# The front of a two-layer decoder step re-staged (a split x tile, squares summed on TensorE), with a convolution, gate chunks, squares and the last stores moved

## The chip, the core and the metric

The kernel runs on one core of a Trainium2 chip. The metric is the device time of one execution in microseconds; the figure for the kernel before is the median of 3 runs. Names used below: PE is TensorE (matmuls), DVE is VectorE, ACT is ScalarE, POOL is GpSimd, SP is SyncE, which issues most of the transfers. PSUM is the memory that matmuls accumulate in; it is divided into banks of 512 fp32 columns.

## The reference, cut to what matters

Two layers (an SSD layer, then a causal pooling layer) over 1024 prompt tokens and 8 x 8 sample tokens, width 1024, and a final RMSNorm. Everything is fp32.

```
def rmsnorm(x, g):
    return x * lax.rsqrt(jnp.mean(x * x, axis=-1, keepdims=True) + EPS) * g
...
    sc = jax.nn.silu(c)
    for i in range(DEPTH):                       # DEPTH = 2
        mod = sc @ ada_w[i] + ada_b[i]
        shift, scale, gate = jnp.split(mod, 3, axis=-1)
        hn = rmsnorm(x, norm_g[i]) * (1.0 + scale[:, None]) + shift[:, None]
        if i % 2 == 0:
            zxbcdt = hn @ w_in                   # gates z, x/B/C and dt
            conv = conv_b + sum(xp[:, k:k + L] * conv_w[k] for k in range(4)); silu(conv)
            y = ssd_scan(...);  out = grouped_rmsnorm(y * silu(z)) @ w_out
        else:
            u, z = split(hn @ w_in)              # windows of 2, 4, 8, 16 tokens summed over u
            out = (pooled @ w_group * ch_scale * silu(z)) @ w_out
        x = x + (1.0 + gate[:, None]) * out
    y = rmsnorm(x, final_norm_g)
```

## The kernel before, in words

Activations lie channel-major: `x` is 8 tiles (k = 0 to 7) of 128 channels by 1088 tokens (1024 prompt, 64 sample). A projection runs over three token chunks `CH` of 368, 368 and 352 columns. Each fp32 factor is held as a rounded part and a remainder (`hh` and `hl` for activations, `wh` and `wl`, or `w` and `w`, for weights), and one product is three matmuls (`mm1`, L189 to L192: hh x wh, hl x wh, hh x wl). ACT makes the rounded part (a copy), DVE or POOL the remainder (a subtraction).

**The front** (`setup`, `front`). SP loads the conditioning `cT`, the eight x tiles, the table `vec` (conv weights, biases, adaLN bias and norm gains), the constants `kc` (with a 9-column selection matrix), `wdt`, and then the adaLN weights, eight blocks of two 512 KB halves, and the input weights `wr`. SP stops at a transfer when eight are under way until the oldest has landed. Meanwhile PE runs 62 matmuls on a tile of ones (`warm`). ACT squares each x tile (L1411, L1415), DVE adds the squares into `rst` (L1416), PE sums `rst` over the 128 channels by a matmul with ones (L302) into `ms`, and ACT takes Ln (L305) and Exp (L318): `rst` is then 1/rms of each token. adaLN block 0 (`ada_block`): eight matmuls of the two halves into a PSUM bank (L261), a copy to `mp` (L266), two selection matmuls (L270), and DVE makes `shf` and `scl` of x tile 0 (L280, L281). `modulate` makes `hh` and `hl` of a tile: DVE x*scl*rst (L325), ACT the rounded `hh` with the shift (L331), DVE the remainder `hl` (L332); the 64 sample columns go through four short operations of their own (L338 to L342). A loop over k then runs 18 matmuls for each x tile into six PSUM banks (two weight tiles `ws`, three chunks, called mm and p in the trace), four matmuls of `pdt` (L1451, the step sizes dt), and the adaLN block of a later tile. What PE executes is strictly in the order in which a scheduler has put it; `issue_after` ties an instruction behind another.

**The conv of tile 12** (`conv`, called for group 6, beside the output product of group 5): a first term on ACT, three taps on DVE (L368), tanh on ACT and two closing multiplications on DVE (L370, L372). Around it DVE also writes `gl`, the remainders of the gated activations (L806), which matmuls L835 wait for.

**The start of the pooling layer.** PE computes two channel tiles u (names pl) and a gate tile z chunk by chunk; `z_tile` is a gate chunk. DVE meanwhile prepares T matrices and remainders (`t`, `hl`, L1006), weight remainders (`w`, L184) and the window sums of `w_sums` (`ws`, L930, L935). The products that follow (`st`, L1078 to L1080) belong to a seven-product (Strassen-like) block scheme.

**The end.** `squares` adds the squares of x for the final norm beside the last output blocks (L1785, L1786). In the last quarter of the tokens the four x tiles that are finished last have their squares kept in `sqs` and summed by PE one by one; then Ln, Exp, and `scale` multiplies the eight tiles by 1/rms and the gain, six on DVE (L1805) and two on POOL (L1803), and stores them two by two on SP's queue (L1806).

## Time and profile before

| what | before |
| --- | --- |
| median of 3 runs (lowest, highest) | 1586.11 us (1586.0, 1587.76) |
| the profiled execution: its own time, its span | 1586.18 us, 1584.0 us |
| PE busy in the span | 1568.2 us, 99% |
| DVE busy | 1302.7 us, 82% |
| ACT busy, POOL busy | 790.8 us, 528.4 us |
| first projection matmul (L190) starts | 24.48 us |
| last matmul of the kernel ends | 1575.88 us |

The profile is one execution on the chip. Its span runs from the first to the last instruction, and 2.18 us of the execution lie outside it. PE is busy for 99% of the span, so the time changes where PE waits, where it does work that could go away, and at both ends. The end of a matmul is modelled, so a start-to-start distance is a better measure of pace than the idle time shown.

### The profile page before, as it was taken

How to read it: one execution, taken by the hardware profiler on the slowest of the kernel's cores; microseconds unless marked ns; L12 is line 12 of the kernel's file. 1: busy time of each engine (PE TensorE's matmuls, PEld its weight loads, DVE VectorE, ACT ScalarE, POOL GpSimd, SP SyncE). 2: the span in 40 equal slices, each digit the busy share in tenths (PEclk: the TensorE clock that was granted, in tenths of full speed). 3: DMA queues.
4: the chain of work that ended last, by engine and by line, in shares of the span. 5: the costliest groups of instructions: out<-in, count | busy, mean ns of one | idle time of the engine just before them, and what ended most of it. 6: DMA issues, size and time to landing. Idle time of an engine off the chain costs nothing.

```text
span 1584.0 us, 30719 instructions
## 1 busy us (share of the span) xinstructions
PE 1568.2 (99%) x11946; PEld 1504.7 (95%) x11946; DVE 1302.7 (82%) x2152; ACT 790.8 (50%) x1512; POOL 528.4 (33%) x558
## 2 busy tenths in 40 slices
PE   9999999999999999999999999999999999999997
PEld 7899999999999899989999999999999999999997
DVE  6874789887899999889888858998889777667886
ACT  6663344466666666665456338533333233233364
POOL 0133556522322413221211242576566530000241
PEclk9999999999999999999999999999999999999999
DMA  9422232355555565678999432232333379565783
GB/s 357 167 102 92 89 113 75 113 186 177 172 165 174 171 198 159 220 256 297 332 340 316 161 134 64 83 126 98 117 116 115 105 252 364 140 180 178 165 168 124
DMA packets 122304, 275.57 MB, mean 174 GB/s; under 512 B 18192, under 2 KB 59312, under 8 KB 122160
## 3 DMA queue, kind: packets, MB, share of 16 engines
q1 hardware_dynamic: 117840, 259.79, 47.9%
q0 software_dynamic: 4032, 12.72, 4.7%
q8 instruction: 94, 1.54, 0.4%
q10 hardware_dynamic: 288, 1.11, 0.2%
q14 instruction: 50, 0.41, 0.1%
HBM read 201.12 MB, written 70.23 MB: 171 GB/s over the span
## 4 chain that ended last, share of the span: by engine, by line
PE 89%; DVE 5%; issue 3%; DMA 2%; ACT 1%; POOL 0%; SPq 0%; DVEq 0%; ACTq 0%; POOLq 0%
PE st L1079 11%; PE st L1080 11%; PE st L1078 11%; PE mm L190 11%; PE mm L191 11%; PE mm L192 11%; PE op L1298 3%; PE op L1299 3%; PE op L1297 3%; PE y L645 2%; PE S L623 2%; PE y L649 2%; PE tr L584 1%; PE am L261 1%; PE tr L581 1%
## 5 line engine op out<-in xcount | busy, mean ns | idle before, releaser
L1080 PE MATMUL st<-hh,w 128*128 128x272 f32 x832 | 240.2, 289 | 0.0
L1078 PE MATMUL st<-hh,w 128*128 128x272 f32 x832 | 240.0, 289 | 0.0
L1079 PE MATMUL st<-hl,w 128*128 128x272 f32 x832 | 240.0, 288 | 0.0
L1080 PE MATMUL st<-t,w 128*128 128x272 f32 x624 | 179.6, 288 | 0.5 <-DVE w L184 0.5
L1079 PE MATMUL st<-t,w 128*128 128x272 f32 x624 | 179.3, 287 | 0.4 <-DVE t L1006 0.4
L1078 PE MATMUL st<-t,w 128*128 128x272 f32 x624 | 179.6, 288 | 0.0
L190 PE MATMUL mm<-hh,wh 128*128 128x368 f32 (+1 forms) x528 | 178.9, 339 | 0.0
L191 PE MATMUL mm<-hl,wh 128*128 128x368 f32 (+1 forms) x528 | 174.0, 330 | 0.0
L192 PE MATMUL mm<-hh,wl 128*128 128x368 f32 (+1 forms) x528 | 173.3, 328 | 0.0
L1078 PEld LDWEIGHTS st<-hh,w 128*128 128x128 f32 x832 | 156.8, 188 | 0.0
L1079 PEld LDWEIGHTS st<-hl,w 128*128 128x128 f32 x832 | 156.7, 188 | 0.0
L1080 PEld LDWEIGHTS st<-hh,w 128*128 128x128 f32 x832 | 156.4, 188 | 0.0
L182 ACT ACTIVATE w<-wr 128x512 fp32r<-128x512 f32 x104 | 65.0, 629 | 165.2 <-PE st L1080 136.2
L631 POOL TENSOR_TENSOR hd<-h,cd 128x256 f32<-128x256 f32 x56 | 46.1, 823 | 290.4 <-DVE h L632 138.4
L1297 PE MATMUL op<-b,w 128*128 128x272 f32 x448 | 129.4, 289 | 0.0
L1298 PE MATMUL op<-b,w 128*128 128x272 f32 x448 | 128.9, 288 | 0.4 <-DVE b L1226 0.4
L1299 PE MATMUL op<-b,w 128*128 128x272 f32 x448 | 129.0, 288 | 0.0
L190 PE MATMUL mm<-gh,wh 128*128 128x368 f32 (+1 forms) x372 | 125.3, 338 | 0.0
L192 PE MATMUL mm<-gh,wl 128*128 128x368 f32 (+1 forms) x372 | 122.3, 329 | 0.0
L191 PE MATMUL mm<-gl,wh 128*128 128x368 f32 (+1 forms) x372 | 122.0, 328 | 0.1
L1080 PEld LDWEIGHTS st<-t,w 128*128 128x128 f32 x624 | 117.3, 188 | 0.7 <-DVE w L184 0.7
L1079 PEld LDWEIGHTS st<-t,w 128*128 128x128 f32 x624 | 117.2, 188 | 0.6 <-DVE t L1006 0.6
(310 smaller groups left out, 4603.1 us busy)
## 6 DMA issues: line engine op xcount, KB each, us to landing
wr<-win SPq DMA_DIRECT2D x48, 512.0 KB, 3.8
wr<-pin SPq DMA_DIRECT2D x32, 512.0 KB, 3.7
acb<-acd SPq DMA_DIRECT2D x60, 256.0 KB, 5.1
wr<-pout SPq DMA_DIRECT2D x28, 512.0 KB, 3.8
x<-x1d SPq DMA_DIRECT2D x24, 544.0 KB, 6.3
x1d<-x SPq DMA_DIRECT2D x22, 544.0 KB, 4.5
wr<-pout POOLq DMA_DIRECT2D x20, 512.0 KB, 5.6
x<-xT SPq DMA_DIRECT2D x16, 544.0 KB, 8.1
```

What stands on the lines that cost most here:

```text
L182: self.last_hi = self.nc.scalar.activation(hi, src, AF.Copy)
L190: nc.tensor.matmul(ps[:, :n], hi[:, k, :], ah[:, a:a + n], start=first, stop=False)
L191: nc.tensor.matmul(ps[:, :n], hi[:, k, :], al[:, a:a + n], start=False, stop=False)
L192: nc.tensor.matmul(ps[:, :n], lo[:, k, :], ah[:, a:a + n], start=False, stop=last)
L623: nc.tensor.matmul(S[:, 256 * i:256 * i + 256], Bt, xde.rearrange("p r q -> p (r q)"), start=True, stop=True)
L631: nc.gpsimd.tensor_tensor(out=hd, in0=h[-1], in1=cd.unsqueeze(2).to_broadcast([P, 4, 64]), op=ALU.mult)
L1078: nc.tensor.matmul(ps[c][:, :QUART], hi[:, k], xh[:, t], start=(k == 0), stop=False)
L1079: nc.tensor.matmul(ps[c][:, :QUART], hi[:, k], xl[:, t], start=False, stop=False)
L1080: nc.tensor.matmul(ps[c][:, :QUART], lo[:, k], xh[:, t], start=False, stop=(k == 3))
L1297: nc.tensor.matmul(ps[:, :QUART], hi[:, k], xh, start=k == 0, stop=False)
L1298: nc.tensor.matmul(ps[:, :QUART], hi[:, k], xl, start=False, stop=False)
L1299: nc.tensor.matmul(ps[:, :QUART], lo[:, k], xh, start=False, stop=k == 7)
```

## The change

The front is written anew. The load of `cT` (145 columns) carries the selection matrix, the adaLN biases and the norm gains in one load too, so that `vec` and `kc` are not needed at the start. x tile 1 is loaded on ACT's queue. x tile 7 comes in two loads (368 and 720 columns) that stand around the second half of adaLN block 0; the first two weight tiles come in two parts each, the first k = 0, 1 alone. Squares of x tiles 0, 2, 4 and 7 go to PE as they are (a ones matmul for each chunk and tile, L1468 of the changed kernel); DVE adds only those of 3, 5 and 6 to tile 1's in `rst`. The roots are taken chunk by chunk, the first of them between the halves of adaLN block 0. The weights are split in three parts, the last on POOL. Tiles 0 and 1 are modulated in three chunks; the products of the sample columns with `rst` are on POOL, for tile 0 the rest of its sample chain too. `pdt` of a tile runs a step later, the last four together at the end. `warm` issues 14 and then 4, 4, 3, 4 matmuls, before 62 and 8.

Elsewhere: the closing of conv tile 12 goes behind the `gl` of group 5's product; gate chunk 1 of the first pooling tile moves behind the third u chunk; the first window sums are tied behind other DVE work; `squares` goes behind the last block's preparation; the last quarter's squares of three tiles are added on DVE instead of PE; and the last stores are eight, one for each tile, alternately on SP's and ACT's queues.

```
 setup:
-        nc.sync.dma_start(ct, io["cT"])
+        nc.sync.dma_start(first, io["cT"])
         for k in range(8):
             t = self.slots.get("x")
-            nc.sync.dma_start(t, io["xT"][k])
+            if k == 7:
+                a = CH[0][1]
+                self.ada_load(0, (0,))
+                nc.sync.dma_start(t[:, :a], io["xT"][k][:, :a])
+                self.ada_load(0, (1,))
+                nc.sync.dma_start(t[:, a:], io["xT"][k][:, a:])
+            else:
+                (nc.scalar if k == 1 else nc.sync).dma_start(t, io["xT"][k])
-        nc.sync.dma_start(self.vec, io["vec"])
-        nc.sync.dma_start(self.kc, io["kc"])
+        self.first_load(0, 2)
-        self.warm(62)
+        self.warm(14)
...
 front:
+            for k in range(7):
+                sq = rst if k == 1 else self.raw_tile()
+                for a, n in CH if k == 6 else ((0, TOK),):
+                    nc.scalar.activation(sq[:, a:a + n], xs[k][:, a:a + n], AF.Square)
+                if k in (0, 2, 4):
+                    for c in range(3):
+                        mm = add_up(c, sq, k)
+                    with after(mm):
+                        self.warm((4, 0, 4, 0, 3)[k], "y")
+                elif k > 1:
+                    for a, n in CH if k == 6 else ((0, TOK),):
+                        added = nc.vector.tensor_tensor(out=rst[:, a:a + n], in0=rst[:, a:a + n], in1=sq[:, a:a + n], op=ALU.add)
...
         for k in range(8):
-            if k < 6:
-                self.ada_first(k + 2)
-            for a, n in CH if k == 0 else ((0, TOK),):
+            for a, n in CH if k < 2 else ((0, TOK),):
                 last = self.modulate(0, k, xs[k], rst, hi, lo, a, n, xs[k][:, a:a + n])
...
+            if k > 1:
+                with after(self.mod_hi.ins):
+                    if k == 2:
+                        for f in firsts:
+                            f[2](4, 8)()
+                    unrounded(k - 1)
...
+            if 0 < k < 5:
+                with after(mm.ins):
+                    mm = step_sizes(k - 1)
...
 modulate:
-            eng = nc.gpsimd if l and k % 2 == 0 else nc.vector
-            eng.tensor_tensor(out=t[:, pn:n], in0=x[:, s], in1=rst[:, s], op=ALU.mult)
+            eng = nc.gpsimd if k % 2 == 0 and (l or k == 0) else nc.vector
+            if l:
+                eng.tensor_tensor(out=t[:, pn:n], in0=x[:, s], in1=rst[:, s], op=ALU.mult)
...
 conv, tile 12 (op_hi and op_lo are the last gh and gl of the output product):
+        if ti == 2 * BESIDE[-1]:
+            with self.tc.issue_after(self.row_evict):
+                tap(1)
+            self.taps_late = lambda: [tap(k) for k in (2, 3)]
+            self.conv_close = close
+            return
...
                     with self.tc.issue_after(self.op_hi), self.tc.issue_after(self.op_lo):
                         self.gate_late()
+                        self.conv_close()
...
 w_sums and the pooling layer's start:
-            with self.tc.issue_after(self.t_last) if p < PLAIN and step == 1 else contextlib.nullcontext():
+            with self.tc.issue_after({1: self.lows[5], 2: self.t_new}[step]) if p == 0 and step < 4 else contextlib.nullcontext():
...
             if c == 1:
-                for i in range(2):
-                    z_tile(0, wz, i, CH[i])
-        z_tile(0, wz, 2, CH[2])
+                z_tile(0, wz, 0, CH[0])
+        for i in (1, 2):
+            z_tile(0, wz, i, CH[i])
...
 the end:
         def squares(d, c):
-            if d and c == 0:
+            with self.tc.issue_after(self.last_block[0]), self.tc.issue_after(self.last_block[1]):
+                if d and c == 0:
...
-                    t = sqs[:, QUART * d:QUART * d + QUART]
-                    nc.scalar.activation(t, x[d][:, a:a + QUART], AF.Square)
-                    sq.append(t)
+                    if d < 3:
+                        square(d, QUART, QUART)
+                    else:
+                        nc.scalar.activation(sqs[:, :QUART], x[d][:, a:a + QUART], AF.Square)
...
-        scale(QUART, QUART, p1, ((4, 5), (6, 7), (0, 1), (2, 3)), (4, 6))
+        scale(QUART, QUART, p1, ((5, 7, 0, 4), (1, 2, 6, 3)), (4, 6), (nc.sync, nc.scalar))
```

PE's order at the start of the program, before: the ones matmuls of `warm`, the three sums of `rst` (ms), adaLN block 0 (am; the last row of it selects through kc), and the first projection matmuls.

```order
L245 MATMUL warm_205<-ones 128x128 x62
L302 MATMUL ms_312<-rst_284,ones 128x368
L302 MATMUL ms_316<-rst_284,ones 128x368
L302 MATMUL ms_320<-rst_284,ones 128x352
L261 MATMUL am_328<-ada_324,scp 32x256 x4
L261 MATMUL am_328<-ada_326,scp 32x256 x4
L270 MATMUL am_328<-kc,mp_337 128x9 x2
L245 MATMUL warm_353<-ones 128x128 x8
L190 MATMUL mm_381<-hh_407,w_13_345 128x368
L190 MATMUL mm_382<-hh_407,w_13_345 128x368
L191 MATMUL mm_381<-hl_408,w_13_345 128x368
```

PE's order at the same place in the changed kernel, from behind the sums of x tile 4 on: mm_238 to mm_240 are the three chunks' sums, raw_287 the squares of x tile 7, ambank the bank of the adaLN blocks.

```order
L1468 MATMUL mm_238<-rst_237,ones 128x368
L292 MATMUL ambank<-ada_194,scp 32x256 x4
L1468 MATMUL mm_238<-raw_287,ones 128x368
L292 MATMUL ambank<-ada_197,scp 32x256 x4
L1468 MATMUL mm_239<-rst_237,ones 128x368
L1468 MATMUL mm_240<-rst_237,ones 128x352
L302 MATMUL ambank<-ct,mp_301 128x9 x2
L1468 MATMUL mm_239<-raw_287,ones 128x368
L1468 MATMUL mm_240<-raw_287,ones 128x352
L272 MATMUL warm_327<-ones 128x128 x4
L190 MATMUL mm_349<-hh_355,w_12_314 128x368
L191 MATMUL mm_349<-hl_356,w_12_314 128x368
```

The sum of chunk 0 closes between the two halves of adaLN block 0, and the sums of chunks 1 and 2 close behind its selection.

ACT's order in the changed kernel, from the modulation of x tile 0 (hh_355; x_179 is x tile 0, x_181 tile 1) to the next adaLN copy (mp_393): rst_237 is the root, w_14 a weight part.

```order
L1472 ACTIVATE rst_237<-mm_240,eps 128x352
L363 ACTIVATE hh_355<-x_179,shf_229 128x368
L350 ACTIVATE rst_237<-rst_237 128x352
L376 ACTIVATE hh_355<-x_179 128x64
L299 ACTIVATE mp_393<-ambank 128x256
L363 ACTIVATE hh_355<-x_179,shf_229 128x288
L363 ACTIVATE hh_419<-x_181,shf_229 128x368 x2
```

The copy mp_393 and the last chunk of tile 0 stand behind the sample columns' hh (128x64), which needs the end of the last root and three operations on POOL.

DVE's order at the first products st of the pooling layer, before: hl are activation remainders, ws window sums, w weight remainders, u and t operands of the products.

```order
L1006 TENSOR_TENSOR hl_11503<-x_10259,hh_11502 128x544
L930 TENSOR_TENSOR ws_12404<-u_11751 128x1222
L184 TENSOR_TENSOR w_12158<-sw_12149,w_12158 128x512
L184 TENSOR_TENSOR w_12169<-wr_12029,w_12169 128x512
L930 TENSOR_TENSOR ws_12406<-ws_12404 128x1220
L935 TENSOR_TENSOR ws_12406<-ws_12406,kc 128x3
L184 TENSOR_TENSOR w_12201<-sw_12149,w_12201 128x512
L1089 TENSOR_TENSOR u_12161<-st_12204,u_12167 128x272
L1006 TENSOR_TENSOR t_12135<-x_10372,t_12135 128x544
```

And in the changed kernel:

```order
L1060 TENSOR_TENSOR hl_11483<-x_10239,hh_11482 128x544
L184 TENSOR_TENSOR w_12138<-sw_12129,w_12138 128x512
L184 TENSOR_TENSOR w_12149<-wr_12009,w_12149 128x512
L184 TENSOR_TENSOR w_12181<-sw_12129,w_12181 128x512
L1144 TENSOR_TENSOR u_12141<-st_12184,u_12147 128x272
L1060 TENSOR_TENSOR t_12115<-x_10352,t_12115 128x544
L1144 TENSOR_TENSOR u_12141<-st_12185,u_12147 128x272
L184 TENSOR_TENSOR w_12212<-wr_12009,w_12212 128x512
L984 TENSOR_TENSOR ws_12384<-u_11731 128x1222
L1144 TENSOR_TENSOR u_12147<-st_12215,u_12147 128x272
L984 TENSOR_TENSOR ws_12386<-ws_12384 128x1220
```

The two window sums moved from ahead of the weight remainders and of t to behind them.

## Rows read from the trace of the kernel before

**Rows 1.** The page: busy time of each engine, share of the span, instructions.

```profile
PE 1568.2 (99%) x11946; PEld 1504.7 (95%) x11946; DVE 1302.7 (82%) x2152; ACT 790.8 (50%) x1512; POOL 528.4 (33%) x558
```

**Rows 2.** Chain that ended last, 14 to 26 us: start, duration, what.

```profile
17.26 0.46 DVE rst L1416
...
18.68 0.58 ACT rst L305
...
19.28 0.51 ACT rst L318
...
21.51 1.17 DVE x L338 x8
```

**Rows 3.** Timeline of ACT, 12 to 24 us.

```profile
12.60 1.11 ACT L1415 ACTIVATE raw<-x 128x1088 f32<-128x1088 f32 x1 [0.30 <-DMA x<-xT]
13.96 1.11 ACT L1415 ACTIVATE raw<-x 128x1088 f32<-128x1088 f32 x1 [0.25 <-DMA x<-xT]
...
21.57 0.38 ACT L266 ACTIVATE mp<-am 128x256 f32<-128x256 f32 x1
...
23.82 1.11 ACT L331 ACTIVATE hh<-x,shf 128x368 fp32r<-128x368 f32 x2 [0.65 <-DVE x L325]
```

**Rows 4.** Timeline of PE, steps of the front: start, duration, operation.

```profile
24.48 0.95 PE L190 MATMUL mm<-hh,w 128*128 128x368 f32 x2
...
45.42 0.43 PE L190 MATMUL mm<-hh,w 128*128 128x368 f32 x1
...
50.55 0.44 PE L190 MATMUL mm<-hh,w 128*128 128x368 f32 x1
...
63.84 0.44 PE L190 MATMUL mm<-hh,w 128*128 128x368 f32 x1
...
67.68 0.44 PE L190 MATMUL mm<-hh,wh 128*128 128x368 f32 x1
```

**Rows 5.** Timeline of PE, 17 to 22 us: sums, adaLN block 0.

```profile
17.76 2.10 PE L302 MATMUL ms<-rst,ones 128*128 128x368 f32 x6 [0.76 <-DVE rst L1416]
...
20.86 0.64 PE L261 MATMUL am<-ada,scp 128*32 128x256 f32 x8 [0.44 <-DMA ada<-adaA]
```

**Rows 6.** Stretches of warm matmuls: length, busy PE, PEld (count), granted clock.

```profile
1.06:4.80 3.74, 3.74 (x17) 3.74 (x18) 1.00 0.73 187
4.80:6.80 2.00, 2.00 (x20) 2.00 (x19) 1.00 1.00 405
```

**Rows 7.** Groups by shape on POOL, 955 to 1000 us: busy, mean ns.

```profile
L339 POOL TENSOR_TENSOR x<-x,scl 128x64 f32<-128x64 f32 x4 | 1.6, 414 | 0.1
```

**Rows 8.** Waits of PE, 685 to 737 us: total, times, longest.

```profile
PE mm L835 <- DVE gl L806: 1.1, 2, 0.8
```

**Rows 9.** Timeline of DVE, 696 to 716 us.

```profile
699.56 1.22 DVE L370 SCALAR_TENSOR_TENSOR xbc<-raw,raw 128x1024 f32<-128x1024 f32 x1
```

**Rows 10.** Waits of PE, 955 to 1030 us.

```profile
PE st L1080 <- DVE w L184: 0.5, 1, 0.5
PE st L1079 <- DVE t L1006: 0.4, 1, 0.4
PE pl L192 <- DVE wl L145: 0.3, 1, 0.3
```

**Rows 11.** Waits of PE, 1545 to 1553 us.

```profile
PE op L1298 <- DVE b L1226: 0.4, 1, 0.4
```

**Rows 12.** Chain that ended last, from 1573 us.

```profile
1574.03 1.85 PE ms L304 x8
```

**Rows 13.** Timelines of ACT, DVE, POOL at the end; last transfers issued.

```profile
1574.14 0.43 ACT L1843 ACTIVATE sq<-x 128x272 f32<-128x272 f32 x1 [1.97 <-DVE x L1282]
...
1576.85 2.54 DVE L1805 SCALAR_TENSOR_TENSOR y<-x,vec,ms 128x272 f32<-128x272 f32 x6 [2.74 <-ACT ms L1792]
...
1577.36 1.49 POOL L1803 TENSOR_TENSOR y<-x,rst 128x272 f32<-128x272 f32 x2 [6.59 <-ACT rst L318]
...
yT<-y SPq DMA_DIRECT2D x4, 272.0 KB, 2.3
```

More of the change, by code (lines that the diff above doesn't have):

```diff
@@ L191, in mm1 @@
         nc.tensor.matmul(ps[:, :n], hi[:, k, :], al[:, a:a + n], start=False, stop=False)
-        nc.tensor.matmul(ps[:, :n], lo[:, k, :], ah[:, a:a + n], start=False, stop=last)
+        return nc.tensor.matmul(ps[:, :n], lo[:, k, :], ah[:, a:a + n], start=False, stop=last)
     def mm3(self, ps, w, acts, ch):
@@ L217, in setup @@
         nc.vector.memset(self.ones, 1.0)
+        self.wfirst = [self.wp.tile([P, 8, P], F32, tag="wr", bufs=3, name=self.name("wr")) for _ in range(2)]
+        self.first_load(0, 2)
         th = self.tp.tile([P, 8, 9], F32, tag="cth", name="cth")
@@ L476, in dt_phase @@
         an = self.gp.tile([P, 1], F32, tag="an", name="an")
[L477 to L478 removed]
+        with self.tc.issue_after(self.mod_hi.ins), self.tc.issue_after(self.mod_x.ins):
+            nc.scalar.activation(an, self.vec[:, V_ALOG:V_ALOG + 1], AF.Exp)
+            nc.vector.tensor_scalar(an, an, -1.0, None, op0=ALU.mult)
         nc.vector.tensor_scalar(dd, uu, 2.0, None, op0=ALU.add)
@@ L1405, in front, with add_up, root @@
         xs = self.xs
+        rst = sl.get("rst")
+        after = self.tc.issue_after
+        ms = [self.mm_tile() for _ in CH]
+        self.ambank, self.pdt = (self.pp.tile([P, 512], F32, tag="tr", bufs=2, name=n) for n in ("ambank", "pdt"))
+        def add_up(c, sq, k):
+            a, n = CH[c]
+            return nc.tensor.matmul(ms[c][:, :n], self.ones, sq[:, a:a + n], start=k == 0, stop=k == 7).ins
+        def root(c):
+            a, n = CH[c]
+            nc.scalar.activation(rst[:, a:a + n], ms[c][:, :n], AF.Ln, bias=self.eps, scale=1.0 / 1024)
+            self.root = self.rstd(rst[:, a:a + n]).ins
@@ new lines, in front, with square, mid @@
+        with self.ln_set():
+            for k in range(7):
[10 more added lines that the diff above has]
+                        added = nc.vector.tensor_tensor(out=rst[:, a:a + n], in0=rst[:, a:a + n], in1=sq[:, a:a + n], op=ALU.add)
+            sq = self.raw_tile()
+            def square(c):
+                a, n = CH[c]
+                return nc.scalar.activation(sq[:, a:a + n], xs[7][:, a:a + n], AF.Square).ins
+            square(0)
+            def mid():
+                with after(self.am):
+                    mm = add_up(0, sq, 7)
+                root(0)
+                return mm
+            with after(mm):
+                mm = add_up(0, rst, 1)
+            blk = self.ada_shift_scale(0, 0, False, mid)
+            with after(mm):
+                next(blk)
+            with after(self.am):
+                for c in (1, 2):
+                    mm = add_up(c, rst, 1)
+            self.adab1 = self.cp.tile([P, 48], F32, tag="adab1", name="adab1")
+            self.cwh = self.gp.tile([P, 160], F32, tag="cwh", name="cwh")
+            with after(added.ins):
+                nc.vector.tensor_scalar(self.adab1, self.va[:, V_ADAB:V_ADAB + 48], 1.0, None, op0=ALU.add)
+            with after(mm):
+                for _ in blk:
+                    pass
+            with after(self.mp.ins):
+                for c in (1, 2):
+                    squared = square(c)
+            self.wslots = []
+            firsts = [self.first_split(t) for t in self.wfirst]
+            with after(squared):
+                lower = [firsts[0][2](0, 2)]
+            for c in (1, 2):
+                with after(self.sel if c == 1 else mm):
+                    mm = add_up(c, sq, 7)
+                with after(squared):
+                    root(c)
+                if c == 1:
+                    with after(self.root):
+                        lower.append(firsts[1][2](0, 2))
@@ L1406, in front @@
+        nc.gpsimd.tensor_tensor(out=xs[0][:, NP:TOK], in0=xs[0][:, NP:TOK], in1=rst[:, NP:TOK], op=ALU.mult)
+        self.hn = []
+        with after(mm):
+            self.warm(4, "y")
+        self.ada_load(1)
+        nc.sync.dma_start(self.vec, io["vec"])
+        self.first_load(2, 8)
+        self.ada_load(2)
+        self.ada_load(3)
         wdts = sl.get("wdt")
@@ L1408, in front @@
         nc.sync.dma_start(wdt, io["wdt"])
[L1409 to L1428 removed]
+        ws = [f[:2] for f in firsts]
         self.wpos = 2
@@ L1453, in front @@
+        unrounded(7)
+        with after(mm.ins):
+            for k in range(4, 8):
+                step_sizes(k)
         sl.free(rst, wdts, *self.wslots)
+        self.sel9, self.va = self.kc[:, K_SEL9:K_SEL9 + 9], self.vec
         dt = self.dt_phase(pdt)
```

202 lines of the change are left out of this document (120 added, 82 removed).

## The prediction

> **What bounds the kernel now.** I read the page first: PE works for 1568.2 us of a span of 1584.0 us [rows 1]. So no other engine's total matters; the time is PE's work plus the places where PE waits or runs filler, and both ends. The waits of PE, stretch by stretch, then show few such places, and the timelines of DVE, ACT and POOL around them say what is late. There are four: the front up to 67.7 us, group 6 of the SSD layer (about 700 us), the start of the pooling layer (about 1000 us), and the end. The change touches each of them, so I cost them one by one. What is gained at one reaches the end, since PE runs without a break between them.
>
> **The front, up to the first projection matmul.** In the chain that ended last the squares' last add ends at 17.72 us, behind `cwh` and `adab1`, which waited for `vec`; then come PE's sums, Ln, Exp, three chunks of each before `mp`, and on DVE eight short products x*rst, 1.17 us, before `shf` [rows 2]. `mp` starts at 21.57 [rows 3] and the first projection matmul at 24.48 [rows 4], 2.9 later.
>
> In the changed order only chunk 0's root stands ahead of `mp`. x tiles land 1.36 us apart, and tile 6 at 13.9 [rows 3]; it stands behind the same bytes as before, give or take 0.1. From there: chunk 0 of its squares 0.5 (a third of 1.11 and a fixed part), DVE's add 0.46 [rows 2], PE's sum of `rst` 0.7 (2.10 for three chunks), the first half of adaLN block 0 0.64, the sum of tile 7's squares 0.7 [rows 5], and some 0.1 at each handover: chunk 0's sum is closed at 17.4. The transfers allow that: 512 KB take 1.28 us at the pace of the x tiles, so the first half of block 0 lands at 15.2, the first part of tile 7 at 15.6, the second half at 16.9. Ln and Exp take 0.58 and 0.51 [rows 2], which gives 18.6 for `mp`, and with the same 2.9 behind it 21.5 for the first projection matmul, 3.0 us earlier. It could be 0.3 better, as `shf` no longer waits for the 1.17 us of products. It could be up to 1.8 worse, if tiles 0 and 1, now in flight together from two queues, both land late: before the sum of `rst`, whose squares are added by 14.9, PE has nine chunk sums of 0.7 and 22 warm passes of 0.1 [rows 6] to do, 8.5 us that start when tile 0's squares are there. Tiles land every 1.36 us, tile 5 at 12.6 [rows 3]: that puts tile 0 at 5.8 and tile 1 at 7.1. With tile 0 at 5.8 and its square of 1.11 the 8.5 us end at 15.4, with both at 7.1 at 16.7. I take 0.5 of that: first projection matmul at 22.0, **2.5 us earlier**. [...]
>
> **The front, the eight steps.** Late steps without an adaLN block take 3.84 us (63.84 to 67.68) and a step with one 5.13 (45.42 to 50.55), so a block costs 1.29 [rows 4]. Eight steps and seven blocks are 39.75; before took 24.48 to 67.68, 43.20, so 3.45 us were lost to waits. In the changed kernel I followed ACT's and DVE's orders through the steps with the durations of before. Where PE waits by that: (a) selection of block 1: its copy stands on ACT behind the sample columns of tile 0, which need the third root (about 23.9) and three dependent POOL operations of 0.41 [rows 7]; the copy ends near 25.9 where PE wants it at 24.9: 1.0. (b) `hl` of tile 0's last chunk, 0.4. (c) tile 1, whose modulation starts on DVE only behind that `hl`: 1.2. (d) tile 2, behind the middle split parts on ACT and DVE and the shift of tile 0: 1.4. (e) the selections of blocks 4 and 6, which stand ahead of a step's matmuls with little between block and copy: 0.7 and 0.4. Together 5.1, 1.7 more than before. The splits of k = 4 to 7 on POOL cost nothing as long as they are done by step 4, some 10 us later. The front gains 2.5 − 1.7 = **0.8**; bounds: 3.3 where the waits stay as they were and tile 0 is early, and −1.5 where tile 0 is late or (c) repeats in steps 3 and 4.
>
> **Group 6.** PE waits 1.1 us in two places for `gl` [rows 8]. DVE works back to back ahead of it, and the closing of conv tile 12 is in that line with 1.22 us [rows 9] and a short second part. Behind the `gl` it no longer delays them by 1.3, which covers both waits. But what follows on PE comes 1.1 earlier as well and meets the same DVE queue, which is not shorter. Bounds 0 and 1.4; I take **0.8**, nearer to the row, since DVE's next products for PE are short.
>
> **Pooling layer.** Three waits are addressed: 0.5 for a weight remainder and 0.4 for `t`, which stood behind window sums [rows 10], and 0.3 for `wl`. The window sums now stand behind both; the third u chunk is computed a gate chunk (24 matmuls) earlier, which gives its evacuation time, and `wl` stands four DVE operations earlier. All three gone is **1.2**; nothing waits for the window sums soon (their result goes to memory). Bounds: 0.4, if DVE, still the same work, is late at the next remainder, and 2.0, since idle shown is less than what a stall costs in start-to-start distance.
>
> **Squares beside the last blocks.** `b` L1226 came 0.4 late behind adds of squares [rows 11]; they now stand behind it: **0.4**, bounds 0 and 0.6.
>
> **The end.** PE sums four tiles' squares in 1.85 us, eight passes [rows 12]; now only one, two passes, 0.46. The fourth tile's square on ACT ends at 1574.57 [rows 13], so its sum cannot start at 1574.03 and ends near 1575.05 rather than 1575.88: 0.8. The three sums that DVE does instead lie in its idle time between the quarter's tiles. Then the stores: before, a pair of tiles was issued when both were ready, the first when POOL's first product was done, some 0.75 (half of 1.49) after POOL's start at 1577.36, while DVE, with six products in 2.54 from 1576.85, had its first tile at about 1577.3 [rows 13]. Now each tile leaves alone, so the first transfer starts 0.8 nearer to its product. The eight still move 1.1 MB, 2.7 us at the pace of the x tiles and about as long as DVE's six products, so the start sets the end. 0.8 + 0.8 = **1.6**; bounds 0.8 (stores of half the size gain nothing) and 2.1.
>
> **Sum.** 0.8 + 0.8 + 1.2 + 0.4 + 1.6 = 4.8. The profiled execution took 1586.18, which is 0.07 over the median 1586.11, so 1581.4 and 1581.3: **1581.3 us**.
>
> **Rivals.** *The front turns dense* (chance 0.23): the short waits of (a) to (e) overlap, as PE always has the other matmuls of a step to do. Its waits stay at 3.45, the front gains 2.5, and the time is 1579.6, with tile 0 early 1578.8. For it: weights and adaLN halves land long before they are needed. Against: ACT's order, in which a copy for PE stands behind a chain of POOL.
>
> *The front gives all back* (0.25): DVE and ACT, not the first matmul, set the steps. They have the same modulation to do as before, in smaller pieces for tile 1, and it cannot start before the roots. Then 67 us stays where it is, and if group 6's waits only move too, the rest is 1.2 + 0.4 + 1.6: 1582.9, and 1584 at the low bounds. That is about within 0.2% (3.2 us), which is what a measurement of this kernel can tell from no change.
>
> *Slower, by the clock of TensorE* (0.07). [...]
>
> **How the numbers follow.** My forecast has 0.45, from 1580 to 1582.9. All bounds at the good end together give 1576.8 (3.3 + 1.4 + 2.0 + 0.6 + 2.1 = 9.4), at the bad end 1586.5; the range of 8 in 10 is 1577.0 to 1585.0, which leaves out the slower case and the extreme of the dense one. Faster by over 0.2% means below 1582.9: the forecast, the dense front and a little of the third case, 0.7; within 0.2%: 0.23; slower: 0.07.
>
> **What the profile would show.** First projection matmul at 21.2 to 23; the front's last step ending (first stream matmul) near 66.9; a wait of PE for `mp` near 25 us and for `hh` or `hl` of tiles 1 and 2; no wait for `gl` at L835's place, none for `w` and `t` at the first `st`; the last ones matmul 0.8 earlier against the preceding x update, and the first of eight stores issued within 0.1 of DVE's first product. Wrong would make it: warm or sum matmuls at half pace behind 6 us, a first half of block 0 landing after 17 us, or a new wait behind group 6's close or the window sums.

## The result, and the profile after

The changed kernel takes 1589.63 us, median of 15 runs (1587.38 to 1591.82), against 1587.07 for the kernel before in 15 runs beside it (1585.42 to 1588.23). The ratio is 1.0017, with a 95% interval of 1.001 to 1.0024: 2.6 us slower, where 1581.3 was forecast and 1585.0 was the upper end of the range. The profiled execution took 1588.05 us, its span is 1586.3, 2.3 more than before.

In what follows each matmul of the changed kernel is set beside the same matmul of before, and the difference of their start times is followed through the span ("behind" when later than before; all times in us). PE is **1.97 behind** at the end of the front, 2.24 at 685, 3.81 at 980 (past group 6), 3.21 at 1030, 3.51 at the last block's products, and the span ends 2.3 behind. So in this pair of executions the front lost 2.0, the way to 980 some 1.6 to 1.9, and the pooling layer and the end gave back 0.6 and 1.2.

The page of the changed kernel, in the columns of [rows 1]:

```profile
PE 1567.1 (99%) x11882; PEld 1499.9 (95%) x11882; DVE 1303.2 (82%) x2146; ACT 790.7 (50%) x1518; POOL 538.6 (34%) x571
```

There are 64 matmuls fewer, with 1.1 us less work, in a longer span: the totals do not show where the time went.

PE's timeline in the front of the changed kernel, which answers to [rows 4, 5, 6] (start, duration, operation, and in brackets the idle time ahead of it with its releaser):

```profile
1.06 6.28 PE L272 MATMUL warm<-ones 128*128 128x128 f32 x28 [1.06 <-DVE ones L225]
7.91 2.10 PE L1468 MATMUL mm<-raw,ones 128*128 128x368 f32 x6 [0.57 <-ACT raw L1479]
...
22.41 0.41 PE L190 MATMUL mm<-hh,w 128*128 128x368 f32 x1
...
62.71 0.65 PE L190 MATMUL mm<-hh,w 128*128 128x368 f32 x3
64.68 0.44 PE L191 MATMUL mm<-hl,w 128*128 128x368 f32 x1 [1.31 <-DVE hl L364]
...
67.36 2.36 PE L1553 MATMUL pdt<-x,wdt 128*32 128x256 f32 x32
69.65 0.44 PE L190 MATMUL mm<-hh,wh 128*128 128x368 f32 x1
```

The first projection matmul starts at 22.41, 2.07 earlier than in [rows 4]; 22.0 was forecast. The first matmul behind the front starts at 69.65 instead of 67.68. Between them lie 47.24 us; the eight steps and seven blocks are 39.75, so **7.5 us were lost in the steps** where 5.1 were counted and before lost 3.45. PE's pace behind the warm-up stayed that of before: the six sums at 7.91 take 2.10 as in [rows 5], the later ones 1.99, and the granted clock is recorded as 1.00 in both.

The waits of PE in the first 75 us (total, times, longest):

```profile
PE mm L191 <- DVE hl L364: 2.2, 3, 1.3
PE ambank L302 <- ACT mp L299: 0.9, 2, 0.5
PE ambank L292 <- DVE scl L313: 0.6, 1, 0.6
```

Idle time understates a stall here: for tile 7's `hl` the trace shows 1.31 idle, and from start to start 1.48 are lost. Measured from start to start, less the usual distance of such matmuls, the foreseen ones are 0.55 at 25.60 for block 1's copy (a), 0.34 at 27.54 (b), some 1.0 at 28.6 to 30.1 (c), some 1.5 at 36 to 39 (d), and 0.6 and 0.7 at 43 to 45 (e), where the products of blocks 4 and 5 wait for each other's results in one bank. Not foreseen is the longest, 1.48 at 63.04: tile 7's `hl`. The timelines of DVE and then POOL show why it is late:

```profile
59.68 1.32 DVE L374 TENSOR_TENSOR x<-x,scl 128x64 f32<-128x64 f32 x1
61.03 1.33 DVE L375 TENSOR_TENSOR x<-x,shf 128x64 f32<-128x64 f32 x1
62.29 2.33 DVE L364 SCALAR_TENSOR_TENSOR hl<-x,shf,hh 128x1024 fp32r<-128x1024 f32 x1
```

```profile
59.27 1.64 POOL L1098 TENSOR_TENSOR sw<-wr 128x512 f32<-128x512 f32 x1 [19.15 <-DMA wr<-win]
60.99 1.29 POOL L1099 TENSOR_TENSOR sw<-sw,wr 128x512 f32<-128x512 f32 x1
62.24 1.29 POOL L1103 TENSOR_TENSOR wr<-wr,wr 128x512 f32<-128x512 f32 x1
```

The two short DVE operations each end about 0.1 behind the weight sum of POOL beside which they start: 61.00 against 60.91, 62.36 against 62.28. They take 1.32 and 1.33 instead of 0.22; the long one behind them, beside the third sum, takes 2.33 instead of 1.28. The rows show that they fall together; front_sums_tied, below, has these sums held back. The kernel before has the same three sums, some 4 us earlier: there they lengthened tile 7's first product (2.33) and one short operation (1.32), but `hl` was done at 62.9, ahead of its matmul, and no matmul waited.

Group 6: waits of PE (in the place of [rows 8]) and DVE's line there (of [rows 9]):

```profile
PE mm L889 <- DVE gl L860: 1.2, 2, 0.8
PE S L673 <- DVE xd L650: 1.1, 1, 1.1
```

```profile
699.43 1.28 DVE L860 TENSOR_TENSOR gl<-gr,gh 128x1088 fp32r<-128x1088 f32 x1
700.63 1.36 DVE L403 SCALAR_TENSOR_TENSOR raw<-raw,cwh,raw 128x1112 f32<-128x1112 f32 x1
...
703.49 1.29 DVE L860 TENSOR_TENSOR gl<-gr,gh 128x1088 fp32r<-128x1088 f32 x1 [0.28 <-ACT gh L859]
...
713.03 1.21 DVE L407 SCALAR_TENSOR_TENSOR xbc<-raw,raw 128x1024 f32<-128x1024 f32 x1
...
714.51 0.67 DVE L650 TENSOR_TENSOR xd<-tr,tkx 128x512 f32<-128x512 f32 x1
```

The waits for `gl` are still there: a tap, moved too, took the closing's place. And the closing itself (713.03) now stands directly ahead of `xd`, for which PE waits 1.1. A third wait, 0.6 for ACT's `raw` (L884, at 705), need not be the conv's: combo below, with the conv where it was, has 0.5 of it.

Waits of PE at the pooling layer, 955 to 1030 us (of [rows 10]):

```profile
PE pl L190 <- ACT hh L376: 0.4, 1, 0.4
PE pl L191 <- DVE hl L377: 0.4, 2, 0.2
PE pl L191 <- DVE hl L361: 0.2, 1, 0.2
```

All three of [rows 10] are gone, and three others came. The end, 1540 us on, waits of PE (of [rows 11, 12]) and then the last of the chain of work that ended last:

```profile
PE ms L336 <- ACT sq L2006: 0.6, 1, 0.6
PE op L1354 <- DVE w L1326: 0.5, 1, 0.5
```

```profile
1577.11 0.51 DVE x L1337
...
1577.65 0.44 ACT sq L2006
...
1578.13 0.74 PE ms L336 x2
...
1579.84 0.50 DVE y L1962
```

One sum of two passes instead of eight, as foreseen waiting for ACT's square. From the start of the last output matmul to the first `y` it is 3.05 instead of 3.57, and from there to the span's end 6.45 instead of 7.15: 1.22 less together.

### The profile page after: what moved, and what is told of

The parts are those of the page before. It is cut to its first block, busy times and chain, and to the rows that moved or that the text cites. A ratio compares the mean times of both kernels' runs of the same rounds, so it can differ in the third digit from the quotient of the medians.

```text
span 1586.3 us, 30625 instructions
## 1 busy us (share of the span) xinstructions
PE 1567.1 (99%) x11882; PEld 1499.9 (95%) x11882; DVE 1303.2 (82%) x2146; ACT 790.7 (50%) x1518; POOL 538.6 (34%) x571
## 4 chain that ended last, share of the span: by engine, by line
PE 87%; DVE 5%; DMA 3%; issue 3%; ACT 1%; POOL 1%; SPq 0%; DVEq 0%; ACTq 0%; POOLq 0%
PE st L1135 12%; PE st L1134 12%; PE st L1133 12%; PE mm L190 11%; PE mm L191 11%; PE mm L192 11%; PE op L1353 2%; PE op L1354 2%; PE op L1352 2%; PE y L695 2%; PE S L673 2%; PE y L699 2%; PE tr L634 1%; PE tr L631 1%; PE am L292 1%
```

## The experiments

Each run gives a ratio to the kernel before on the same chip, with its 95% interval. The theories in the expectations: that the losses are those of the places changed, and add up; theory 2, that a late front by itself costs more further on; theory 3, that fewer instructions on PE shift the loads of its code onto a transfer; theory 4, that POOL's weight sums hold DVE in the front's last step; theory 5, that the waits at 43 to 45 us come from issuing adaLN blocks 4 and 5 together. What is read of traces is of one profiled execution of each run, and "behind" means behind the profiled execution of before. The first runs take the change apart.

**front_only**: the new front; group 6, pooling layer, squares and end as before.

> The changed front alone; convolution, gate chunks, squares and the end as before. Theory 1 (the parts add up as the two traces read side by side, front +2.0 us, group 6 +1.9, pooling layer -0.6, squares +0.3, end -1.3): 2.0 us over the kernel before, the first stream matmul behind the front near 69.6 us. Theory 2 (group 6 loses only because the front hands over later, in another phase to the transfers): 3.9 over the kernel before. By the prediction's sum it would be 0.8 under it.

1591.0 against 1586.08 us: 1.0032 (1.0019 to 1.0044), more than either theory said. PE is 2.37 behind at the end of the front, as expected, and **5.62 behind at 980**, though nothing in between was changed. The loss is at group 6. The same kernel again (**front_again**), later beside front_wide:

> The same kernel as front_only, beside front_wide on the same chip. Theory 3: the code load again at 680, acb's first use more than 5.8 after its issue, group 6 loses 1.5 to 3, and 3.6 to 5 over the kernel before. If what it loses there is chance, group 6 loses under 1.3 this time and the time is 2.5 over.

1590.93 against 1586.45: 1.0033 (1.002 to 1.0046); 2.10 behind, then 4.29.

**g6_undone**: the changed kernel with the conv's closing and taps where they were.

```
...
-                        self.conv_close()
...
```

> The changed kernel with the taps, the closing and the weights of group 6 ordered as before. Theory 1: 1.9 us under the changed kernel, 0.5 to 0.7 over the kernel before, and no wait of PE for xd at the place where it stood 1.1. Theory 2: as slow as the changed kernel, 2.5 over the kernel before. The prediction's sum: 0.8 over the changed kernel.

1588.23 against 1586.08: 1.0015 (1.0007 to 1.0024), 2.15 us over where theory 1 said 0.5 to 0.7. The wait for `xd` is gone, but PE goes from 2.51 behind at 685 to 4.63 at 980: the order of the conv is not what the front's own loss at group 6 comes from.

**rest_only**: before with the pooling layer, squares and end of the diff. **end_only**: before with the diff's last part, the end, alone.

> The kernel before with the pooling layer's order, the squares and the end changed; front and group 6 as before. Theory 1: 1.6 us under the kernel before. By the prediction's sum 3.2 under it. Theory 2 says nothing else here than theory 1.

> The kernel before with the changed end alone (three squares added on VectorE, eight single stores on two queues). Theory 1: 1.3 us under the kernel before; by the prediction 1.6 under it. If the second queue cost what the smaller stores save: 0.5 under it, from the shorter sum on TensorE alone.

1584.68 and 1585.04 against 1586.08: 0.9994 (0.9985 to 1.0003) and 0.9996 (0.9987 to 1.0005): 1.4 and 1.0 under, and neither told from no change. The trace of end_only shows only half of what the changed kernel gains at its end: 0.51 from the sum, as there, and nothing from the stores, with 7.23 us from the first `y` to the span's end (rest_only 7.15, before 7.15).

**What happens at group 6.** A queue of instruction loads (q8) moves 16 KB at a time, mostly every 13 to 20 us. I take it for PE's code, since its loads move when little but PE's matmuls is changed (front_wide below: 7.3 us behind the issue instead of 0.2 ahead of it). Without the 64 matmuls and their weight loads these loads fall elsewhere. SP's issues (start, duration), DMA records of 679 to 680.5 us, ACT's wait, and PE's waits of 685 to 737 us in front_only:

```profile
680.53 1.18 SPq L119 DMA_DIRECT2D wr<-wout  x1
681.81 0.97 SPq L599 DMA_DIRECT2D acb<-acd  x2
```

```profile
q8 instruction: 1, 0.02, 4.3%
```

```profile
689.18 0.63 ACT L616 ACTIVATE ea<-acb 128x512 f32<-128x512 f32 x1 [6.13 <-DMA acb<-acd]
```

```profile
PE y L721 <- DVE xbc L658: 1.3, 1, 1.3
PE S L747 <- DVE xbc L658: 1.0, 1, 1.0
```

And SP's and ACT's in the kernel before:

```profile
678.06 0.37 SPq L119 DMA_DIRECT2D wr<-wout  x1
678.52 0.97 SPq L556 DMA_DIRECT2D acb<-acd  x2
```

```profile
683.62 0.63 ACT L573 ACTIVATE ea<-acb 128x512 f32<-128x512 f32 x1 [3.05 <-DMA acb<-acd]
```

In front_only a code load (q8) lies on SP's issue of `wr`, which takes 1.18 instead of 0.37, and ACT gets `acb` 7.4 us behind its issue instead of 5.1. What follows (`ea`, POOL's state update, DVE's taps beside it) is late, and PE waits for it. In the kernel before, loads lie 3.8 ahead of that issue and 8.8 behind it. In the eight kernels in which a load begins at most 0.55 us ahead of that issue (the changed kernel, front_only, front_again, g6_undone, front_split_dve, front_sums_late, front_sums_tied, combo) the issue took 0.83 to 1.27, and `acb` came 5.1 to 7.9 behind its own; in the eleven others 0.37 or 0.38, and 5.1 to 6.2. So the issue tells the two groups apart, and `acb` does so in part: in five of the eight it came later than in any of the eleven.

**before_shift**: before with 44 of its 62 warm matmuls as 11 of 512 columns (`wide`), in the same time, to bring its loads there.

```
-        self.warm(62)
+        self.warm(18)
...
+        for _ in range(11):
+            nc.tensor.matmul(ps, self.ones, wide, start=True, stop=True)
```

> The kernel before, with 44 of its 62 warm matmuls replaced by 11 of four times the columns: PE is busy just as long, but executes 66 matmuls and 66 weight loads fewer, so the loads of its code (16 KB transfers about every 16 us) fall elsewhere between the other transfers. Theory 3 (with the changed front such a load meets the transfer of acb at 680 us, ACT, POOL and DVE behind it are late, and group 6 loses 1 to 3 us): the load moves from 674 to about 680, ACT's first use of acb comes 1 us or more later, group 6 loses 1 to 2.5 us and the time is that much over the kernel before. Theory 2 (the late front): group 6 and the time as in the kernel before, within 0.5 us.

1586.48 against 1586.48: 1.0002 (0.9994 to 1.0011). The load fell 5.7 behind `wr`'s issue, not on it, so this says nothing on theory 3. It shows something else: with front and group 6 as before, PE goes from 0.49 ahead at 400 us to 0.82 behind at 685 and 1.87 behind at 980.

**front_shift**: front_only with its 29 warm matmuls as 61 of 64 columns, to move the loads back.

```
-        self.warm(14)
+        self.warm(30, n=64)
...
```

> The changed front alone (as in front_only), with its 29 warm matmuls replaced by 61 of half the columns: 64 matmuls and weight loads more, as many as the kernel before has. Theory 3: the code load falls near 676.5 and 689 instead of 680, group 6 loses at most 0.5 instead of 2.7, and the time is 2.0 to 2.5 under front_only, 2.4 over the kernel before (the front's own loss, which stays). Theory 2: as front_only, 5 over.

1601.56 against 1586.48: 1.0098 (1.0083 to 1.0112). `acb` had no collision and group 6 lost 0.8, but the start was slow. Six sums behind the warm passes, and the next six:

```profile
13.92 3.53 PE L1461 MATMUL mm<-raw,ones 128*128 128x368 f32 x6
...
19.01 2.05 PE L1461 MATMUL mm<-raw,ones 128*128 128x368 f32 x6
```

PE's 60 warm passes (two for each matmul) stood 0.213 apart to 13.7 us, and the front ended 12.8 behind.

**front_wide**: the same aim with wide warm matmuls, 40 passes fewer of the same total.

```
...
-        for _ in range(n):
-            self.nc.tensor.matmul(ps[:, :128], self.ones, self.ones, start=True, stop=True)
+        for n in [128] * (m % 4) + [512] * (m // 4) if m != 3 else [384]:
+            self.nc.tensor.matmul(ps[:, :n], self.ones, self.wide[:, :n], start=True, stop=True)
```

> The changed front alone, its 29 warm matmuls made of 2 of 128, 6 of 512 and 1 of 384 columns: the same columns, 20 matmuls and weight loads (40 passes) fewer, so a code load that fell at 680 us falls 4 to 6 us later and no longer on the issue of the weights ahead of acb. Theory 3 (the code load at 680 makes acb late and group 6 loses): the issue takes 0.4 instead of 0.8 to 1.2, ACT's first use of acb comes at most 5.8 after acb's issue, group 6 loses under 1.3, the time is 2.5 to 3.5 over the kernel before. Rival (it is the transfers' own order behind the changed front, or chance): as front_only, 3.6 to 5 over.

1589.05 against 1586.45: 1.002 (1.0012 to 1.0029). SP's issue and ACT's wait:

```profile
680.38 0.37 SPq L119 DMA_DIRECT2D wr<-wout  x1
```

```profile
685.99 0.63 ACT L618 ACTIVATE ea<-acb 128x512 f32<-128x512 f32 x1 [3.10 <-DMA acb<-acd]
```

The front ends 2.26 behind and PE is still 2.36 behind at 980. With the same steps, 1.9 us less than front_again in the same set of runs: **theory 3 holds for the front alone**. How much a collision costs varies: of the runs with this front and a collision, front_only lost 3.0 from 685 to 980, front_again 1.9 and front_sums_late (below) 1.1, and before_late, without one, 1.0.

**before_late**: before with 2 us of matmuls, three of 512 columns, behind the front's last.

```
+            for _ in range(3):
+                nc.tensor.matmul(ps, self.ones, wide, start=True, stop=True)
```

> The kernel before with three matmuls of 512 fp32 columns (0.85 us each, 2.6 in all) behind the front's last pdt, so that everything behind the front comes 2.6 us later; front and all else as before but for the order of some ACT and DVE work up to 120 us. Theory 2 (behind a late front the transfers meet otherwise and group 6 loses another 2 to 2.7): 4.5 to 5.3 over the kernel before. Rival (a late front costs its lateness and no more; what front_only lost in group 6 comes with where its code loads or its transfers fall): 2.6 over, group 6 within 1 of before.

1588.63 against 1586.99: 1.0013 (1.0004 to 1.0022). 2.10 behind at the front, 3.08 at 980, 2.24 at the end: theory 2 falls, the late front costs about what it is late.

**The front's steps.** front_split_dve puts the last weight parts on DVE instead of POOL; front_sums_late orders POOL's weight sums behind tile 7's `hl` in the issue order; front_sums_tied makes them wait for it by data; front_ada_spread issues one adaLN block a step, as before. All have the rest as front_only.

```
...
-(self.nc.gpsimd if a == 4 else self.nc.vector)
+self.nc.vector
...
+            with self.tc.issue_after(self.front_last):
...
+                tied = nc.gpsimd.tensor_copy(d, self.front_lo).ins
...
-                for i in ((3,), (4, 5), (6,), (7,))[k - 1]:
+                    self.ada_first(k + 2)
...
```

> The changed front alone, with the remainders for k = 4 to 7 of the first two weight tiles made on DVE instead of POOL. Theory 4 (DVE stands while POOL works on these 512-wide operands: short DVE operations of 0.22 take 1.31 beside them at 37 to 40 us, and steps 3 and 4 wait for it): these take 0.22 again, DVE is 2.2 less 1.4 for the two splits = 0.8 ahead, the waits of PE near 42.7 and 44.0 shrink by about that, the front ends 0.5 to 1.0 earlier than in front_only. Rival (the waits near 43 come from the selections of blocks 4 and 5, which share one bank): no change, or 0.3 later for the added work.

1590.07 against 1586.48: 1.0023 (1.0013 to 1.0033). The front ends 2.05 behind, 0.05 to 0.3 better than in the two executions of front_only; from the first projection matmul to the front's end it is 46.86 instead of 47.25. DVE's short operations at 37 to 40 us take 0.22 again, but the waits at 43 to 45 us are unchanged, so the rival of the expectation holds for these.

> The changed front alone, with POOL's first weight sums (59 to 63.5 us) tied behind the modulation of x tile 7 on DVE. Theory 4: DVE's two short operations of tile 7 take 0.22 instead of 1.32 and its hl 1.28 instead of 2.33, PE's wait of 1.3 for that hl near 64.7 is gone, the front ends 1.2 to 1.5 us earlier than in front_only; what stands on DVE behind it (the T matrices) is slower, without a wait of PE. Rival (DVE is late by its own work there): the wait stays, 0 to 0.3 us.

1590.32 against 1586.48: 1.0025 (1.0015 to 1.0034). POOL's sums still ran at 59.80, behind 19.3 us without work on POOL: the order of issue did not hold them there. It stands as one more run of front_only, with a collision (the issue took 0.83, `acb` came 5.6 behind its own).

> The changed front alone, POOL's first weight sums now made to wait by data: a one-element copy on POOL reads the end of x tile 7's hl first. (front_sums_late had moved them in the order only; POOL still ran them at 59.8 us.) Theory 4 (DVE stands while POOL works): PE's wait of 1.3 for hl near 65 us is gone, the front ends at 68.3 instead of 69.7, DVE's work behind it takes longer. Rival: the wait stays.

1591.95 against 1586.99: 1.0035 (1.0022 to 1.0049). DVE in the last step:

```profile
60.69 0.22 DVE L374 TENSOR_TENSOR x<-x,scl 128x64 f32<-128x64 f32 x1
60.95 0.23 DVE L375 TENSOR_TENSOR x<-x,shf 128x64 f32<-128x64 f32 x1
62.00 1.29 DVE L364 SCALAR_TENSOR_TENSOR hl<-x,shf,hh 128x1024 fp32r<-128x1024 f32 x1 [0.83 <-ACT hh L363]
```

The short operations are short again, PE's 1.3 wait is gone, and from the first projection matmul to the front's end it is 45.69 instead of 47.25, so 1.56 less: **theory 4 holds**. The front ends only 1.43 behind, since its first matmul was late at 23.42 in this execution. The time is no better, as this kernel collides too (`wr` 1.27, `acb` 7.5) and loses 4.0 at group 6.

> The changed front alone, with one adaLN block for each step (blocks 3 to 7 behind steps 1 to 5) instead of blocks 4 and 5 together. Theory 5 (PE waits 0.9 and 0.7 near 43 to 45 us since the selection of block 4 stands right behind its products, and block 5 behind that in the same bank): both waits gone, the front ends 1.2 to 1.6 earlier than in front_only, near 68.2. Rival (the steps are bound by DVE and ACT, and the wait moves to the next hh or hl): at most 0.4 earlier.

1595.62 against 1586.99: 1.0055 (1.0043 to 1.0068). Between 40 and 50 us no wait is left, so theory 5 is right about these waits, but block 7 and tile 7 came late, and with them `hl` met POOL's sums:

```profile
PE mm L191 <- DVE hl L364: 4.1, 3, 3.2
```

The front ends 7.0 behind, where the expectation had 1.2 to 1.6 of gain. combo, the next run, holds POOL's sums back and still takes 50.1 us for its steps with the blocks spread, against 45.7 in front_sums_tied: gathering the blocks early is the better order.

**combo**: the changed kernel with four of these edits at once: group 6 undone, blocks spread, sums tied and splits on DVE.

> The changed kernel with group 6 ordered as before, one adaLN block for each step, POOL's first weight sums tied by data, and the remainders for k = 4 to 7 on DVE. If the three repairs of the front add up (1.4 + 1.4 + 0.3), its end is at 66.6, 1.1 earlier than before, and with the gains of the pooling layer and the end the time is 2 to 3 us under the kernel before; if they do not, 0 to 1 over it.

1591.03 against 1586.99: 1.0028 (1.0017 to 1.004); 5.29 behind at the front.

**after_wide**: the changed kernel with front_wide's warm matmuls. **repaired**: that with sums tied, group 6 undone, and the gate chunk back:

```
             if c == 1:
-                z_tile(0, wz, 0, CH[0])
-        for i in (1, 2):
-            z_tile(0, wz, i, CH[i])
+                for i in range(2):
+                    z_tile(0, wz, i, CH[i])
+        z_tile(0, wz, 2, CH[2])
```

> The whole changed kernel with only its warm matmuls reshaped as in front_wide (40 passes fewer, same columns). Theory 3: the code load no longer meets the issue ahead of acb, acb's first use within 5.8 of its issue, and the time falls by 1.2 to 2 against the changed kernel, to 0.6 to 1.4 over the kernel before. If the collision costs nothing in the whole kernel: 2.6 over, as the changed kernel.

> The changed kernel with the reshaped warm matmuls, POOL's first weight sums tied behind x tile 7 by data, group 6 and the gate chunks ordered as before. By the parts measured so far: front +1.3, window sums -1.2, squares -0.6, end -1.3: 1.8 under the kernel before, about as best. If the wait for tile 7's hl is only traded for later ones, as in front_sums_tied: 0 to 1 under.

1588.54 and 1587.27 against 1586.72: 1.0015 (1.0006 to 1.0024) and 1.0005 (0.9996 to 1.0014): 1.8 and 0.55 us over. after_wide lies between its two expectations, and by its interval it can't be told from the changed kernel. Waits at group 6 in after_wide, 685 to 737 us:

```profile
PE S L675 <- DVE xd L652: 1.1, 1, 1.1
PE mm L891 <- DVE gl L862: 0.8, 1, 0.8
```

`acb` is on time (5.15) and the moved closing costs its 1.1 all the same: this wait is the moved conv's and not the collision's. From 2.85 behind at 685 PE goes to 2.84 at 720 and 3.91 at 760; in between it waits 1.3 for the state `h` (at 738.9), whose cause no run shows. With the collision alone (g6_undone) PE lost 2.1 from 685 to 980, with the moved conv alone 0.85, with both (the changed kernel) 1.55: the two don't add up. repaired, expected 0 to 1.8 under, is not told from before by its interval; its profiled execution started late (first projection matmul 24.86) and lost 1.6 from 685 to 980 without a collision.

**best**: before with the window sums, squares and end of the diff, and no moved gate chunk.

> The kernel before with the order of the window sums, the squares and the end changed; front, group 6 and the gate chunks as before. In rest_only moving the gate chunk made waits of 0.45, 0.55 and 0.45 near 987 to 994 us and took away 0.32 and 0.47: a net loss of 0.7. Expected: those waits gone, those for w and t (0.66 and 0.58) still gone, 2 us under the kernel before. If the gate chunk's move had no part in it: 1.4 under, as rest_only.

1584.77 against 1586.45: 0.9991 (0.9983 to 1.0), where 2 us under was expected. The two stalls at 1018 and 1023 us gave 0.66 and 0.58, and behind them a wait of 0.7 for a weight remainder of POOL's came at 1048:

```profile
PE st L1081 <- POOL w L184: 0.7, 1, 0.7
```

Its median is 1.7 us under that of before, and the interval reaches no change. Its stores gained nothing (7.11 from the first `y` to the end).

## Why the prediction was wrong

**The front (0.8 gain forecast, 2.0 lost).** The first projection matmul came 2.07 earlier for the 2.5, but this pair flatters it: `mp` started at 19.18 for 18.6, and the profiled execution of before was a late one. In the five other runs with the old front the matmul starts at 23.70 to 24.01, in nine others with the new one at 22.53 to 22.86 (in two more, front_sums_tied and repaired, at 23.42 and 24.86), so some 1.1 was gained as a rule. The step that failed is "the eight steps": 7.5 us of waits for 5.1. This is no matter of the execution: from the first projection matmul to the front's end it is 43.2 in the runs with the old front (before_late, with its added matmuls, apart) and 47.0 to 47.4 in those with the new one and its steps unchanged. The list (a) to (e) was right, some 4.7 together, with (a) at 0.55 for 1.0 and (e) at 1.3 for 1.1. It lacked tile 7's `hl`, 1.48: I priced only POOL's splits, which "cost nothing as long as they are done by step 4", and never set POOL's later weight sums beside DVE's operations; front_sums_tied shows that cause. It also lacked the `hl` of tile 0's first chunk (0.38, at 22.41); some 0.9 is left over, in short distances. The four `pdt` now stand together at the end instead of filling waits; what this costs was not tried alone. This is the rival "the front gives all back", only further.

**Group 6 (0.8 gain forecast, 1.6 to 1.9 lost).** Two failures. "Behind the `gl` it no longer delays them" took out one operation and did not see that a tap moves up into its place, nor what stands behind the closing's new place: `xd`, 1.1 (gone in g6_undone, and there without a collision in after_wide). And no rival had the code loads: with the changed front alone they cost 1.2 to 2.3 by medians (front_sums_late, front_again and front_only against front_wide, each as its excess over before). That `acb` has so little slack was in the trace of before, 3.05 of waiting on ACT, and was not read.

**Pooling layer (1.2 forecast).** The stalls for `w` and `t` went, 0.66 and 0.58, and those for `u` on ACT and for `wl`, 0.32 and 0.47; but the gate chunk had been cover for the sample columns' `hh` and `hl`, which now cost 0.45, 0.55 and 0.45. Net 0.6 at 1030, 0.4 at 1300, the low bound. Without the gate chunk's move (best) the gain up to 1030 is 1.2 to 1.5 and about 1.0 of it is lost at 1048.

**Squares (0.4).** Not settled: PE's start there came 0.32 earlier in the changed kernel and 0.60 in rest_only and best, but also 0.60 in before_late, which has the old squares. The 0.63 of new wait up to 1545.4 appears in front_wide too (0.90), without the moved squares, so it isn't theirs.

**The end (1.6 forecast, 1.22).** The sum was right in mechanism, 0.52 for 0.8, and it is the same in every run that has it. The stores were not: "the start sets the end" failed. The first store is issued 0.53 instead of 1.29 behind the first `y`, as foreseen, but the last one 2.94 instead of 3.03, and the bytes have landed 5.16 behind it instead of 5.50. Nor is the 0.70 the stores' alone. From the first `y` to the span's end it is 7.11 to 7.23 with the new stores and the old front (end_only, rest_only, best), 7.15 to 7.16 with both old, 6.90 to 6.96 with the new front and the old stores (eight runs), and 6.44 to 6.46 with both new (five runs). In the three runs without a gain an 8 KB load of code (another queue, q14) lies 3.7 to 4.5 behind the first `y`, among the last transfers, and in the five with both new none does. That it takes the gain away was not tried.

**The clock** rival did not occur. No run shows its term, steps at a lower pace: in the changed kernel the matmuls of 368 columns stand 0.16 to 0.17 apart ahead of the longest wait (1.48, at 63.04) and, from the second on, behind it. A slow start was shown instead. In the changed kernel the 28 warm passes stood 0.213 apart up to 7.3 us, with no loss, as the sums behind them waited 0.57 for their squares; in front_shift six sums at 13.92 took 3.53 and the next six, at 19.01, 2.05, and the front ended 10.4 later than in front_only.

**In sum**, front, the way to 980, pooling layer, squares and end: −2.0 − 1.8 + 0.6 − 0.3 + 1.2 = −2.3, the span's difference. By medians the front alone is 4.5 to 4.9 over (2.6 without the collision) and the rest 1.4 under (rest_only), together some 3.1 to 3.5 against 2.6 for the whole, which the intervals allow. The premise "What is gained at one reaches the end" did not hold: end_only was 0.79 ahead at 70 us and level at 680, in unchanged code. Open is why the start of the front varies between executions of like kernels (22.4 to 24.9 us), and why unchanged code moves, by 0.7 to 1.3 later between 400 and 685 us (before_shift, end_only, rest_only) and by up to 1 either way around 685 to 980 (+1.0 in before_late and before_shift, −0.5 in best). This is as large as most terms of my sum, and group 6's 1.6 to 1.9 of a single pair is known no better than that.

## What to carry to other kernels

Before moving an operation off a wait, read what moves up into its old place and who waits behind its new one; and set short DVE operations on the path against POOL's wide ones: here two of 0.22 took 1.32 and 1.33 beside weight sums of 1.64 and 1.29, and each ended about 0.1 behind one. Removing instructions from an engine can shift code loads far behind the place: 40 warm passes fewer in the first 22 us (front_wide) put the one at 680 us 7.3 behind SP's issue instead of 0.2 ahead of it. Where a transfer is waited for already, look at what the instruction queue moves at its issue. And try a part of the change alone before its gain in the whole is put down to it: the new stores gained nothing with the old front.

## What the runs showed that was not expected

- Where a 16 KB code load fell on an issue of SP, that issue took 0.83 to 1.27 us instead of 0.37 (eight kernels against eleven); in five of the eight the transfer behind it came 6.4 to 7.9 us behind its own issue, later than in any of the eleven (5.1 to 6.2). In front_ada_spread the load fell on the issue of `acb` itself, which took 1.59 instead of 0.42.
- In front_shift 60 warm passes of 64 columns stood 0.213 us apart for 13 us, with the granted clock recorded as 1.00 all the while, and six sums behind them took 3.53 us instead of 2.05. Behind 17.3 us the same passes stood 0.112 apart. In the changed kernel 28 passes of 128 columns stood 0.213 apart too, and its first six sums behind them, at 7.91, took 2.10.
- DVE operations of 64 columns took 1.32 and 1.33 us beside POOL's sums of 512, and 0.22 and 0.23 where these were held back (front_sums_tied).
